# Norm steps, key parts, latent copies and the last two latent heads of a streaming encoder step, rearranged

## The chip, the cores and the metric

The kernel runs on one core of one Trainium2 chip. The metric is the device time of one execution in microseconds (us). The core has a matmul engine (TensorE, PE in the profile; PEld are its weight loads, which overlap the matmuls), three engines for elementwise work (VectorE: DVE, ScalarE: ACT, GpSimd: POOL), and SyncE (SP), whose queue issues most DMA transfers. Each engine takes its own instructions in order and waits on semaphores for the others.

## The reference

One layer of an encoder is applied to two streams: a prompt of 16 meta tokens and 512 rows, and a sample of 64 new rows with 128 cached rows behind it. Width 2048, float32. The core of it:

```python
h = rmsnorm(x, norm_attn_g)
qd, kd, vd, qm, ckv, krope = project(h)           # one matrix w_in; norms and rope on the latent parts
# 8 differential heads, two softmaxes each
p = softmax(qd0 . kd0 + bias) - lam * softmax(qd1 . kd1 + bias)
o_d = rmsnorm(p @ vd, diff_subln_g) * (1 - lam_init)
# 8 latent heads: keys and values expanded from ckv
km, vm = expand_latent(ckv)
o_m = softmax((qn . km + qr . krope) * scale) @ vm
x = x + concat(o_d, o_m) @ w_out
h = rmsnorm(x, norm_ffn_g)
x = x + (silu(h @ gate) * (h @ up)) @ down
y = rmsnorm(x, final_norm_g)                      # also returned: new keys, values, latents, roped keys
```

Keys are visible by chunks of 64 rows.

## The kernel before

Rows are kept as columns: an operand tile is 128 features by up to 592 tokens (64 sample rows, 512 prompt rows, 16 meta rows). For float32 accuracy every operand is split into a high part (ScalarE copies it to a rounded type, lines 156 and 160) and a low part (VectorE subtracts, lines 153 and 161); a product is three matmuls, high-high, high-low and low-high (`mm3`, line 183). Weights arrive by DMA in a tile `wr`, and are split into `wh` and `wl`.

The work has these stages.

- Start (lines 361 to 518): the input is loaded, turned by TensorE in 16 blocks (`transpose_x`), split, and multiplied with the first head's query and key weights block by block (`project_both`). Loads are issued by SyncE in the order of lines 407 to 413. In blocks 11 and 12 two products for the bias table ride along (`bias_part`), in block 15 a transpose of the gains (`gains_part`); VectorE copies both out of the spare half of the block's PSUM tile. After block 13 the row factors of the first norm are worked out on VectorE and ScalarE (`rc`, lines 502 to 506); `row_factors` then spreads them with ten small matmuls (`prb`) and a VectorE copy (`rb`). It stands behind block 14. After block 15 comes the value projection of head 0 (`psv`).
- Eight differential heads (lines 537 to 771): for each head three projections of 16 blocks (96 matmuls each). Between their blocks runs the attention of the head before. `new_keys` evacuates the key projection and stacks high and low halves (`stack_keys`, two parts for each of two ranges); `keys` and `natural` turn keys for the output. `diff_attend` makes scores into two banks ("sp"), which VectorE reduces (line 626) and ScalarE exponentiates (line 630), then calls `probabilities_times_values`, then squares the output, sums it by TensorE (`pq`), applies a reciprocal root (`rsqrt`, lines 165 to 169) and the gain (line 669).
- Latents (lines 773 to 893): norm and rope of the latent rows; five times three transposes `pn` go through the single bank "tp", are copied by VectorE (`nn`, line 882) and stored.
- Latent heads and first half of the mixing (lines 918 to 1110): eight heads (`latent_attend`), each with scores and then `probabilities_times_values` through the banks "tp" (one) and "po" (one). A head's values wait for the whole chain of the head before (`att2[h - 1]`, line 1081). `mix_out` multiplies the differential outputs with the first half of `w_out`; it has the last rank, and so fills what the heads leave.
- Second half of the mixing (lines 1250 to 1301): latent outputs are read back (`m`, three buffers with tag "x"), split to `mh` and `ml`, and multiplied (line 187); the first gate weights `raw0` are loaded.
- The feed-forward layer (from line 1303): gate, up and down products in a Winograd form, then the last norm.

TensorE's order up to line 1115 is planned when the program is built: `Streams` runs generators against a planned clock `now`, which only TensorE's instructions advance. A generator yields a planned time to wait, a list of others to wait for, or takes a PSUM bank (`take`) that another gave back with a delay (`give`). Of those ready, the one with the lowest rank goes on. TensorE's instructions are pinned in that order by `keep_in_program_order` (an instruction is issued after all that was traced before it on its engine; it need not wait for them to finish). The other engines' instructions, and the DMA issues, are ordered by a scheduler at build time, by its own estimate of when each is ready.

## Time and profile before

| | us |
|---|---|
| median of 3 runs | 2391.92 (2391.61 to 2392.06) |
| profiled execution | 2392.82 |
| its span, first to last instruction | 2390.9 |
| mean granted TensorE clock | 0.995 |

Windows of the profile are in us from the span's start. Roughly, the start takes 0 to 55, the differential heads 55 to 480, the latents to 530, the latent heads to 771, the second half of the mixing to 875, and the feed-forward layer the rest.

A row of the timeline has the start, the duration, engine, line, operation, the tiles written and read, their shapes, the count of instructions merged in it, and in brackets how long the engine had been idle and which instruction released it. A row of the windows has the stretch, its length, and for each engine its busy time and its number of instructions, then the granted TensorE clock (1.00 is full), the DMA share and GB/s. A row of the waits has who waited for whom, the total, the number and the longest. Matmuls are pipelined, so the durations of neighbours overlap.

### The profile page before, as it was taken

To read this page: it belongs to the slowest core of one execution; us is meant where nothing else is said; L and a number is where in the kernel's file an instruction comes from. 1 tells how busy PE (TensorE), PEld (TensorE's weight loads), DVE (VectorE), ACT (ScalarE), POOL (GpSimd) and SP (SyncE) were. 2 spreads that over 40 slices of the span, in tenths; PEclk is the share of its full clock that TensorE was granted. 3 is DMA by queue.
4 is the path that set the end of the run, shared out by engine and by line. 5 is a ranking of instruction groups with operands and counts; after the bars stand their busy time and mean duration, and the time that the engine had idled before them with its cause. 6 is when DMAs were issued, how large, how long until landed. Compare 5 with 4: busy or idle time off the path is not lost. (4 is left out here: it accounts for less than half of the span.)

```text
span 2390.9 us, 43556 instructions
## 1 busy us (share of the span) xinstructions
PE 2341.0 (98%) x17318; PEld 2304.9 (96%) x17318; DVE 1883.8 (79%) x2742; ACT 1128.1 (47%) x2000; POOL 738.6 (31%) x457
## 2 busy tenths in 40 slices
PE   8999999999998999999999999999999999999998
PEld 7999999989998999999999999999999999999997
DVE  6566777676674789888888888888888788899884
ACT  6454555344454554444444444444444333333435
POOL 1000000130000455555555554554554222222220
PEclk9999999999999999999999999999999999999999
DMA  9432333263323643444345345445445984654522
GB/s 277 110 92 83 93 98 94 66 177 104 113 86 124 185 146 119 141 156 160 126 156 165 128 149 166 132 145 166 139 139 185 321 284 152 231 172 151 189 89 97
DMA packets 361513, 353.09 MB, mean 148 GB/s; under 512 B 23719, under 2 KB 318414, under 8 KB 361310
## 3 DMA queue, kind: packets, MB, share of 16 engines
q1 hardware_dynamic: 359038, 345.78, 45.8%
q0 software_dynamic: 992, 3.48, 0.5%
q8 instruction: 136, 2.23, 0.4%
q10 hardware_dynamic: 1280, 1.06, 0.2%
q14 instruction: 67, 0.55, 0.1%
HBM read 268.82 MB, written 82.34 MB: 147 GB/s over the span
## 5 line engine op out<-in xcount | busy, mean ns | idle before, releaser
L1240 PE MATMUL m<-b,wh 128*128 128x288 f32 x7280 | 1061.9, 294 | 7.0 <-ACT wh L156 3.7
L1240 PEld LDWEIGHTS m<-b,wh 128*128 128x128 f32 x7280 | 995.5, 188 | 10.2 <-ACT wh L156 6.8
L1244 PE MATMUL m<-b,wl 128*128 128x288 f32 x3640 | 583.0, 296 | 3.7 <-DVE wl L153 2.7
L153 DVE TENSOR_TENSOR wl<-raw,wh 128x1024 fp32r<-128x1024 f32 (+2 forms) x347 | 511.1, 1474 | 39.4 <-ACT wh L156 37.3
L1244 PEld LDWEIGHTS m<-b,wl 128*128 128x128 f32 x3640 | 514.4, 188 | 9.2 <-DVE wl L153 8.2
L156 ACT ACTIVATE wh<-raw 128x1024 fp32r<-128x1024 f32 (+2 forms) x347 | 313.5, 904 | 364.5 <-PE m L1240 318.7
L1226 POOL TENSOR_TENSOR ws<-raw 128x512 f32<-128x512 f32 (+2 forms) x124 | 226.9, 1830 | 614.9 <-DVE wl L153 367.5
L156 ACT ACTIVATE wh<-ws 128x512 fp32r<-128x512 f32 (+2 forms) x248 | 196.6, 793 | 286.0 <-PE m L1240 120.0
L153 DVE TENSOR_TENSOR wl<-ws,wh 128x512 fp32r<-128x512 f32 (+2 forms) x248 | 249.9, 1008 | 8.1 <-PE m L1244 4.4
L108 PE MATMUL ps<-xh,wh 128*128 128x296 f32 (+1 forms) x992 | 223.9, 307 | 2.2 <-DVE ls L635 1.2
L108 PE MATMUL ps<-xl,wh 128*128 128x296 f32 (+1 forms) x992 | 216.4, 300 | 0.2
L108 PE MATMUL ps<-xh,wl 128*128 128x296 f32 (+1 forms) x960 | 208.3, 298 | 0.5 <-DVE wl L153 0.5
L1390 DVE TENSOR_TENSOR c<-c,s 128x288 fp32r<-128x288 f32 x172 | 171.2, 995 | 0.0
L108 PEld LDWEIGHTS ps<-xh,wh 128*128 128x128 f32 x992 | 161.1, 191 | 5.7 <-ACT wh L156 2.6
L1498 DVE TENSOR_TENSOR y<-y,m 128x288 f32<-128x288 f32 x280 | 125.8, 450 | 49.8 <-PE m L1244 49.7
L108 PEld LDWEIGHTS ps<-xl,wh 128*128 128x128 f32 x992 | 161.7, 190 | 1.1 <-DVE xl L161 1.0
L108 PEld LDWEIGHTS ps<-xh,wl 128*128 128x128 f32 x960 | 156.4, 190 | 0.7 <-DVE wl L153 0.7
L1226 POOL TENSOR_TENSOR raw<-raw 128x1024 f32<-128x1024 f32 (+1 forms) x46 | 141.8, 3084 | 3.5
L153 DVE TENSOR_TENSOR wl<-wr,wh 128x1024 fp32r<-128x1024 f32 (+1 forms) x109 | 115.7, 1061 | 33.1 <-ACT wh L156 30.4
L156 ACT ACTIVATE wh<-wr 128x1024 fp32r<-128x1024 f32 (+1 forms) x111 | 101.8, 917 | 75.7 <-PE ps L108 55.8
L1336 DVE TENSOR_TENSOR c<-c,m 128x288 f32<-128x288 f32 x171 | 73.2, 448 | 79.3 <-PE m L1244 40.6
L1409 POOL TENSOR_TENSOR c<-c,rb 128x576 f32<-128x576 f32 x44 | 74.8, 1699 | 138.0 <-ACT c L1408 138.0
(363 smaller groups left out, 3022.0 us busy)
## 6 DMA issues: line engine op xcount, KB each, us to landing
raw<-in_ffn_w_gate SPq DMA_DIRECT2D x44, 1024.0 KB, 6.1
raw<-in_ffn_w_up SPq DMA_DIRECT2D x44, 1024.0 KB, 7.7
b<-opspill SPq DMA_DIRECT2D x147, 288.0 KB, 6.1
raw<-in_ffn_w_down SPq DMA_DIRECT2D x32, 1024.0 KB, 5.4
wr<-in_w_in SPq DMA_DIRECT2D x57, 512.0 KB, 4.0
opspill<-s SPq DMA_DIRECT2D x43, 576.0 KB, 3.1
opspill<-c SPq DMA_DIRECT2D x43, 576.0 KB, 6.8
raw<-in_ffn_w_down SPq DMA_DIRECT2D x8, 1280.0 KB, 6.2
```

What stands on the lines that cost most here:

```text
L108: self.tc.keep_in_program_order(self.pe.matmul(out, lhsT, rhs, start=start, stop=stop))
L153: V.tensor_tensor(lo, src, f32(hi), op=ALU.subtract)
L156: S.activation(hi, src, AF.Copy)
L1226: (G if p in (5, 7) else V).tensor_tensor(x, y, z, op=ALU.add if p == 5 else ALU.subtract)
L1240: PE.matmul(banks[p], wh[:, k, :], x, start=first and new and k == 0 and x is hi, stop=False, skip_group_check=not new)
L1244: PE.matmul(banks[p], wl[:, k, :], hi, start=False, stop=last and k == n - 1, skip_group_check=not new)
L1336: V.tensor_tensor(c, c, banks[p], op=ALU.add)
L1390: V.tensor_tensor(src[:, k].bitcast(F32R), src[:, k], f32(hi[:, k]), op=ALU.subtract))
L1409: G.tensor_tensor(g[:, f, :], g[:, f, :], rb2, op=ALU.mult)
L1498: V.tensor_tensor(c, c, banks[p], op=ALU.add)
```

## The change

- The second weight group is loaded ahead of the last 1024 columns of the own rows, the one-hot table and the bias. `row_factors` goes behind block 15. The copies of bias and gains go behind the block's split and copy.
- In heads 0 to 6 the three VectorE steps of the output norm and the gain are each issued 2.0 of planned time apart, and pinned behind what was traced on VectorE before (`rsqrt_apart`, `behind`). The parts of `stack_keys` move from `new_keys` into `keys`, 1.0 apart, their subtractions pinned likewise. The bank of `natural`'s first transposes is given back after 2.9 in place of 1.9.
- The copy `nn` is made by ScalarE.
- The weights of the first mixing block are asked for at block 11 of the last projection (`late`).
- The last latent head waits for the head before the one before it, and goes beside head 6: it uses the banks "sp" and "ps" in place of "tp" and "po", the freed query tiles `cqh` and `cql` for its buffers, a `pm` of its own (cleared by GpSimd), and steps 2.0 of planned time apart.
- In the second half of the mixing four of the eight input tiles use the four buffers "xg"; the load of `raw0` is pinned behind what SyncE was given before.

The diff, cut to its core:

```diff
+    def behind(ins):
+        return tc.keep_in_program_order(ins)
+
+    def rsqrt_apart(r, v, pace):
+        S.activation(r, v, AF.Ln)
+        S.activation(r, r, AF.Exp, scale=-0.5)
+        yield pace
+        behind(V.tensor_tensor(v, v, r, op=ALU.mult))
+        yield pace
+        behind(V.scalar_tensor_tensor(v, v, -0.5, r, op0=ALU.mult, op1=ALU.mult))
+        yield pace
+        behind(V.scalar_tensor_tensor(r, v, 1.5, r, op0=ALU.add, op1=ALU.mult))
+        yield pace
...
-    def project(ps, wsrc, xs, ready=None, n=TH):
+    def project(ps, wsrc, xs, ready=None, n=TH, late=None):
...
+                if late and kc == 11:
+                    late()
                 yield 0
...
+    def rotating(pool):
+        def made(name, cols):
+            if name == "p5x":
+                return pool.tile([P, cols], F32R, name=name)
+            return [pool.tile([P, cols], F32R, name=name + s, tag="pk" + s, bufs=2) for s in "hl"]
+        return made
...
                 if cg == 1:
+                    load_own(slice(512, 1024), load)
+                load_both(4 * cg, 4, (load, load))
+                if cg == 1:
+                    load_own(slice(1024, D), load)
                     load(oh, c_onehot)
                     load(rbt, rel_bias)
-                    load_own(slice(512, D), load)
-                load_both(4 * cg, 4, (load, load))
...
-                if kc in (11, 12):
-                    bias_part(kc - 11, spare)
-                elif kc == KC - 1:
-                    gains_part(spare)
+                rider = {11: bias_part, 12: bias_part, KC - 1: gains_part}.get(kc)
+                if rider:
+                    rider(kc - 11, spare)
                 xt = xn.tile([P, T], F32, name="xt", tag=f"xt{kc % 12}")
                 split_scaled(xh[kc], xl[kc], sp, gA[:, kc:kc + 1])
                 V.tensor_copy(xt, sp)
                 store(xspill[kc], xt[:, 0:TQ])
+                if rider:
+                    {bias_part: bias_row, gains_part: gains_out}[rider](kc - 11, spare)
...
-                if kc == KC - 2:
-                    row_factors()
+            row_factors()
...
-            st.give("tp", 1.9)
+            st.give("tp", 2.9)
...
-            yield 2.0
+            for new, old in NEW:
+                for part in stack_keys(kk, new, z[:, old]):
+                    yield 1.0
+            yield 1.0
...
-                V.tensor_tensor(kk[c][half[1 - c], cols], src[half[c]], f32(kk[c][half[c], cols]), op=ALU.subtract)
+                behind(V.tensor_tensor(kk[c][half[1 - c], cols], src[half[c]], f32(kk[c][half[c], cols]),
+                                       op=ALU.subtract))
+                yield
...
-            rsqrt(r, sq)
-            V.scalar_tensor_tensor(o32, o32, g08, r, op0=ALU.mult, op1=ALU.mult)
             if h < H - 1:
+                yield from rsqrt_apart(r, sq, 2.0)
+                behind(V.scalar_tensor_tensor(o32, o32, g08, r, op0=ALU.mult, op1=ALU.mult))
                 store(mspill[h], o32)
+            else:
+                rsqrt(r, sq)
+                V.scalar_tensor_tensor(o32, o32, g08, r, op0=ALU.mult, op1=ALU.mult)
...
-                for new, old in NEW:
-                    stack_keys(kk[h % 2], new, z[:, old])
...
-                    yield from project(ps, w_in[:, off:off + P], xs1, n=QH if i < 4 else TH)
+                    yield from project(ps, w_in[:, off:off + P], xs1, n=QH if i < 4 else TH,
+                                       late=(lambda: mixed.append(mix_weights(0))) if i == 3 else None)
...
-                V.tensor_copy(nn[0:n], pn[0:n, 0:320])
+                S.activation(nn[0:n], pn[0:n, 0:320], AF.Copy)
...
-                wh, wl = weights(w_out[0:1024, i * P:(i + 1) * P].rearrange("(k p) c -> p k c", p=P), 8, P)
+                wh, wl = mixed.pop() if mixed else mix_weights(i)
...
-            yield [valued[h // 2]] + ([att2[h - 1]] if h else [])
+            beside = h == H - 1
+            yield [valued[h // 2]] + ([att2[h - 1 - beside]] if h else [])
...
+            if beside:
+                home = lambda tag, dtype: aq[0].tile([P, TQ], dtype, name="pv" + tag, tag=tag)
+
+                def made(name, cols):
+                    if name == "p5x":
+                        return aq[0].tile([P, cols], F32R, name=name, tag="e", bufs=2)
+                    return [home(f"cq{s}{name[2]}", F32R)[:, 0:cols] for s in "hl"]
+
+                o32, pm = home("cql3", F32), home("cqh3", F32R)[0:80, 0:512]
+                banks = ("sp", sbank), ("ps", lambda: pjt()[:, 0])
+                G.memset(f32(pm), 0.0)
+            else:
+                o32, pm = zx.tile([P, TQ], F32, name="o32", tag="o32"), shared["pm"]
+                made, banks = rotating(aq[0]), (("tp", tbank), ("po", obank))
             yield from probabilities_times_values(
...
-                o32, 2, {})
+                pb, p5, pm, shared["vm"][:, c], [(vh[:, 1 + t, c], vl[:, 1 + t, c]) for t in range(4)],
+                vh[:, 0, c], (vh[:, 5, c], vl[:, 5, c]), made, *banks, 2.0 if beside else 0.0,
+                o32, {})
...
-        m = ma.tile([P, TQ], F32, name="x", tag="x", bufs=3)
+        m = ma.tile([P, TQ], F32, name="x", **(dict(tag="xg", bufs=4) if 3 <= h < 7 else dict(tag="x", bufs=3)))
...
-            raw0 = load_raw(rw, w_gate, 0, 8, 0, 1, "ws")
+            raw0 = load_raw(rw, w_gate, 0, 8, 0, 1, "ws",
+                            lambda dst, part: tc.keep_in_program_order(nc.sync.dma_start(dst, part)))
```

In `probabilities_times_values` the pool and bank arguments become `made` (which hands out the split tiles) and two pairs of a bank's name and its maker; its steps are the same.

More of the change, by code (lines that the diff above doesn't have):

```diff
@@ L227, in stack_own, with probabilities_times_values @@
         V.tensor_tensor(v[NS:P], src, f32(v[0:NS]), op=ALU.subtract)
-    def probabilities_times_values(pt_b, p5, pm, vm, vkeys, vown, vpast, pool, tbank, pso, pace, o32, bufs, transposed):
+    def probabilities_times_values(pt_b, p5, pm, vm, vkeys, vown, vpast, made, tbank, pbank, pace, o32, transposed):
         def evac(name, src, rows, cols):
-            hi = pool.tile([P, cols], F32R, name=name + "h", tag="pkh", bufs=bufs)
-            lo = pool.tile([P, cols], F32R, name=name + "l", tag="pkl", bufs=bufs)
+            hi, lo = made(name, cols)
             split(hi[0:rows], lo[0:rows], src[0:rows, 0:cols])
@@ L239, in times_values @@
                 PE.matmul(po[:, c0:512], a, b, start=False, stop=(n == 3 and m == 2))
-        yield from st.take("po")
-        po = pso.tile([P, 512], F32, name="po", tag="po")
-        yield from st.take("tp")
-        tp = tbank()
+        yield from st.take(pbank[0])
+        po = pbank[1]()
+        yield from st.take(tbank[0])
+        tp = tbank[1]()
         for b in range(4):
@@ L250, in probabilities_times_values @@
         last = []
-        st.give("tp", 2.2)
+        st.give(tbank[0], 2.2)
         for t in range(2):
             yield pace
-            yield from st.take("tp")
+            yield from st.take(tbank[0])
             w = 512 - P * t
-            tp = tbank()
+            tp = tbank[1]()
             for b in range(t, 4):
@@ L264, in probabilities_times_values @@
             last = [(t, (hi, lo), t * P)]
-            st.give("tp", 2.2)
+            st.give(tbank[0], 2.2)
         yield pace
-        yield from st.take("tp")
-        tp = tbank()
+        yield from st.take(tbank[0])
+        tp = tbank[1]()
         for n, (t, b) in enumerate(((2, 2), (2, 3), (3, 3))):
@@ L274, in probabilities_times_values @@
         last = [(2, (hi[:, 0:256], lo[:, 0:256]), 256), (3, (hi[:, 256:384], lo[:, 256:384]), 384)]
-        st.give("tp", 1.7)
+        st.give(tbank[0], 1.7)
         yield pace
-        yield from st.take("tp")
-        tp = tbank()
+        yield from st.take(tbank[0])
+        tp = tbank[1]()
         for n in range(2):
             PE.transpose(tp[:, n * P:(n + 1) * P], p5[:, n * P:(n + 1) * P], ident)
-        p5x = pool.tile([P, 2, 2, NS], F32R, name="p5x")
+        p5x = made("p5x", 4 * NS).rearrange("p (a b c) -> p a b c", a=2, b=2)
         split(p5x[:, 0], p5x[:, 1], tp[:, 0:2 * P].rearrange("p (a b) -> p a b", a=2)[:, :, 0:NS])
@@ L286, in probabilities_times_values @@
         S.activation(o32[:, NS:TQ], po, AF.Copy)
-        st.give("tp", 1.7)
-        st.give("po", 1.2)
+        st.give(tbank[0], 1.7)
+        st.give(pbank[0], 1.2)
         yield pace
-        yield from st.take("po")
-        po5 = pso.tile([P, 512], F32, name="po", tag="po")
+        yield from st.take(pbank[0])
+        po5 = pbank[1]()
         vh, vl = vpast
@@ L298, in probabilities_times_values @@
         V.tensor_tensor(o32[:, 0:NS], o32[:, 0:NS], po5[:, NS:2 * NS], op=ALU.add)
-        st.give("po", 1.0)
+        st.give(pbank[0], 1.0)
+    def rotating(pool):
[4 more added lines that the diff above has]
+        return made
     def ev(ps, n=TH):
@@ L340, in tbank, with obank @@
             return pst.tile([P, 512], F32, name=name, tag="tp")
+        def obank(name="po"):
+            return pso.tile([P, 512], F32, name=name, tag="po")
         def ztile(name="z"):
@@ L427, in bias_part, with bias_row @@
                 PE.matmul(bank[0:H], rbt, oh[:, cols[i]], start=True, stop=True)
+            def bias_row(i, bank):
                 trs = ztile("trs")[0:H, 0:NREL // 2]
@@ L433, in bias_part, with gains_part, gains_out @@
                         G.dma_start(tsk[h], trow[h:h + 1, :].to_broadcast([P, NREL]))
-            def gains_part(bank):
+            def gains_part(i, bank):
                 PE.transpose(bank[:, 0:P], gains, ident)
+            def gains_out(i, bank):
                 V.tensor_copy(gT, bank[:, 0:rows])
@@ L567, in keys @@
             PE.transpose(pk[:, 0:P], ck, ident)
-            stack_keys(kk, slice(T, TP), pk[:, 0:P])
+            for part in stack_keys(kk, slice(T, TP), pk[:, 0:P]):
+                pass
             st.give("tp", 1.5)
@@ L1084, in latent_attend @@
             c = slice(i * P, (i + 1) * P)
-            o32 = zx.tile([P, TQ], F32, name="o32", tag="o32")
+            if beside:
[10 more added lines that the diff above has]
+                made, banks = rotating(aq[0]), (("tp", tbank), ("po", obank))
             yield from probabilities_times_values(
-                pb, p5, shared["pm"], shared["vm"][:, c], [(vh[:, 1 + t, c], vl[:, 1 + t, c]) for t in range(4)],
-                vh[:, 0, c], (vh[:, 5, c], vl[:, 5, c]), aq[0], tbank, pso, 0.0,
-                o32, 2, {})
+                pb, p5, pm, shared["vm"][:, c], [(vh[:, 1 + t, c], vl[:, 1 + t, c]) for t in range(4)],
+                vh[:, 0, c], (vh[:, 5, c], vl[:, 5, c]), made, *banks, 2.0 if beside else 0.0,
+                o32, {})
             store(mspill[8 + h], o32)
```

7 lines of the change are left out of this document (5 added, 2 removed).

## The prediction

> **What bounds the kernel now.** I read the page's first part, then the table of stages, then TensorE's waits, then the short stretches around them.
>
> ```profile
> span 2390.9 us, 43556 instructions
> ...
> PE 2341.0 (98%) x17318; PEld 2304.9 (96%) x17318; DVE 1883.8 (79%) x2742; ACT 1128.1 (47%) x2000; POOL 738.6 (31%) x457
> ```
>
> TensorE is the bound: 49.9 us of 2390.9 are left without a matmul, and the change removes no matmul. It can only win back idle time, and time in which matmuls ran slowly. The table of stages says where these are (columns: stretch, length, then busy time and instructions of PE, PEld, DVE, ACT, POOL, then granted clock, DMA share, GB/s).
>
> ```profile
> 0.00:60.00 60.00, 49.44 (x326) 45.74 (x327) 39.83 (x65) 36.41 (x75) 8.80 (x22) 0.97 0.92 277
> ...
> 190.00:205.00 15.00, 11.61 (x74) 11.31 (x74) 11.68 (x30) 7.22 (x17) 0.00 (x0) 0.89 0.25 75
> 205.00:505.00 300.00, 298.56 (x2218) 294.30 (x2218) 210.35 (x467) 150.40 (x313) 25.88 (x22) 1.00 0.36 100
> 505.00:530.00 25.00, 19.93 (x125) 17.65 (x125) 17.81 (x26) 9.15 (x15) 6.50 (x7) 0.93 0.53 141
> ...
> 744.00:782.00 38.00, 31.74 (x194) 27.84 (x193) 15.20 (x25) 14.50 (x27) 0.00 (x0) 0.87 0.51 161
> ...
> 930.00:2391.00 1461.00, 1445.13 (x10773) 1430.55 (x10771) 1244.92 (x1454) 665.82 (x1035) 613.12 (x333) 1.00 0.50 163
> ```
>
> Four short stretches (start, 190 to 205, 505 to 530, 744 to 782) hold 25.3 us of the idle time and all of the lowered clock. The feed-forward part from 930 on idles 15.9 us, and the change does not touch it. TensorE's waits name the causes (who waits for whom: us, times, longest).
>
> ```profile
> PE pn L112 <- DVE nn L882: 3.6, 3, 1.9
> PE sp L108 <- DVE nm L626: 3.4, 1, 3.4
> ...
> PE prb L108 <- DVE rc L169: 2.5, 1, 2.5
> ...
> PE ps L108 <- DVE wl L153: 1.9, 2, 1.5
> ...
> PE ps L108 <- DVE ls L635: 1.2, 1, 1.2
> ...
> PE pnb L112 <- ACT na L564: 0.5, 1, 0.5
> ```
>
> **The clock doubles some of these waits.** The half-clock stretches lie on one grid of 3.41 us; so I asked for the stretches of that grid.
>
> ```profile
> 47.81:51.23 3.42, 0.95 (x9) 0.80 (x8) 1.88 (x7) 1.33 (x6) 1.14 (x5) 1.00 0.93 334
> 51.23:54.64 3.41, 3.41 (x17) 3.41 (x16) 1.53 (x2) 0.00 (x0) 0.00 (x0) 0.50 1.00 363
> 194.59:198.00 3.41, 1.91 (x15) 1.67 (x13) 3.29 (x5) 1.44 (x4) 0.00 (x0) 1.00 0.56 154
> 198.00:201.41 3.41, 1.52 (x10) 1.52 (x11) 2.91 (x12) 1.35 (x5) 0.00 (x0) 1.00 0.53 168
> 201.41:204.83 3.42, 3.42 (x16) 3.36 (x15) 1.76 (x7) 1.38 (x5) 0.00 (x0) 0.50 0.00 0
> ...
> 447.17:450.58 3.41, 3.41 (x27) 3.41 (x26) 3.16 (x9) 0.73 (x2) 0.00 (x0) 1.00 0.62 161
> ...
> 522.27:525.68 3.41, 1.66 (x9) 0.93 (x9) 3.38 (x7) 1.45 (x3) 0.00 (x0) 1.00 0.68 197
> 525.68:529.09 3.41, 3.41 (x16) 3.41 (x16) 2.42 (x4) 0.00 (x0) 0.00 (x0) 0.50 0.67 193
> ...
> 768.03:771.44 3.41, 1.84 (x13) 1.38 (x11) 1.03 (x3) 2.22 (x6) 0.00 (x0) 1.00 0.03 9
> 771.44:774.85 3.41, 3.15 (x14) 3.11 (x14) 1.58 (x3) 0.96 (x3) 0.00 (x0) 0.50 0.84 273
> ```
>
> Idle for 2.47, 1.89, 1.75 or 1.57 us of 3.41 (length less PE busy), and the next stretch runs at 0.50. Idle for 1.50 (194.59 to 198.00), and the next is at 1.00. A half-clock stretch gets through 16 matmuls where a full one gets through 27, so it costs 11/27 of 3.41, about 1.4 us. A wait of some 1.6 us in one stretch thus costs 1.6 plus 1.4.
>
> [...]
>
> **The change part by part.**
>
> *Order of the first loads (lines 407 to 413).*
>
> ```profile
> 20.16 1.04 ACT L156 ACTIVATE wh<-wr 128x1024 fp32r<-128x1024 f32 x1
> ...
> 21.25 0.54 PE L108 MATMUL ps<-xh,wh 128*128 128x288 f32 x2 [1.00 <-ACT wh L156]
> ```
>
> The two transfers of the second weight group move ahead of two thirds of the own rows, the one-hot table and the bias on SyncE's queue: four issues (oh, rbt, two of xo) go behind two of wr, some 0.4 MB, which at the 277 GB/s of the first stage is 1.5 us. The split at 20.16 stands behind ScalarE's squares, without an idle mark before it, so its place in the queue decides and not the data alone. TensorE lost 1.00 us there and 0.46 for the other half (the 1.9 of the waits less its longest). Between 0 and 1.5; I take **1.0**, as an earlier transfer lets the scheduler put the split earlier. What goes later is read from the eighth block on, over 8 us on.
>
> *Row factors one block later (lines 507 to 508), bias and gain copies behind the splits.*
>
> ```profile
> 47.56 0.43 PE L108 MATMUL ps<-xh,wl 128*128 128x296 f32 x2
> 50.46 1.69 PE L108 MATMUL prb<-ident,rc 128*128 128x128 f32 x10 [2.47 <-DVE rc L169]
> 52.19 0.78 DVE L445 COPY rb<-prb 128x592 f32<-128x592 f32 x1 [1.87 <-PE prb L108]
> ...
> 54.82 0.44 PE L108 MATMUL ps<-xh,wh 128*128 128x296 f32 x2
> ```
>
> Block 14 ended at 47.99. Block 15's twelve products, 1.5 us by the 27 in 3.41 and some 0.3 until the last is out, fill most of the wait to 50.46; the factors then start near 50.4. Their ten matmuls took 1.69 partly at half clock; I take 1.2. New: the value projection comes right behind, and its bank is probably the one that the factors leave, so it waits for the 0.78 us copy, 0.9 with its start. It starts at 52.5 in place of 54.82: **2.3**, with the clock in it (3.2 if the bank is another; 1.5 if the chain is late by 0.8). The copies moved (0.5 us each on VectorE) are the same work later, behind a split that TensorE needs first.
>
> *Norm steps and key parts at a distance (lines 167 to 169, 577, 668 to 669, 700 to 701).*
>
> ```profile
> 194.32 0.75 DVE L167 TENSOR_TENSOR sq<-sq,r 128x576 f32<-128x576 f32 x1
> ...
> 199.40 0.43 DVE L626 CUSTOM_DVE_ANT_0 e<-sp,bias 128x272 f32<-128x272 f32 x1
> ```
>
> Between these, VectorE ran four norm steps and four key subtractions in a row, and the score reduction, whose matmuls were done by then, stood behind them. Both score banks were full, and TensorE waited 3.40. With steps 2.0 and key parts 1.0 of planned time apart, each kept behind what was traced before it, the reduction goes ahead of them: 3.40 and one half-clock stretch, at most 4.8; I take **4.6**. The added planned time (some 8 us for a norm, 3 for keys) ends in nothing urgent: the norm's result is only stored, for the mixing stage, and keys are wanted when the value projection's 96 matmuls are done, some 12 us by the 27 in 3.41 above. The 1.2 us of ps on ls (an evacuation behind norm steps) may go or stay: **0.6**. The longer lease of the transpose bank (2.9 for 1.9) takes away most of the 0.5 before pnb: **0.4**.
>
> *Turned latents copied by ScalarE (line 882), first mixing weights asked for at block 11 (line 921).*
>
> ```profile
> 509.57 0.76 DVE L761 TENSOR_TENSOR zl<-ps,rb 128x576 f32<-128x576 f32 x1 [0.83 <-PE ps L108]
> ...
> 511.38 5.06 DVE L161 SCALAR_TENSOR_TENSOR cql<-zl,gT,cqh 128x576 fp32r<-128x576 f32 x4
> 516.36 0.47 DVE L882 COPY nn<-pn 80x320 f32<-80x320 f32 x1
> ...
> 521.29 1.06 ACT L156 ACTIVATE wh<-wr 128x1024 fp32r<-128x1024 f32 x1 [8.86 <-PE ps L108]
> ...
> L564 ACT ACTIVATE na<-pna x8: 572/580/601, 62.8 to 395.0; 128x512 f32<-128x512 f32 x8
> ```
>
> The copy stands behind 5.06 us of VectorE work while ScalarE idles for 8.86 us. On ScalarE it costs about the same (the last row, from the view of line 564: eight copies of 128x512, 572 to 601 ns) and starts when its transposes are done. All 3.6 us of waits on nn go, and the stretch at 525.68. What is late next: VectorE's four splits now end near 516, and the query products that read them come near 520. The first mixing weights' low half, traced a third of a projection earlier, can be made in VectorE's 0.8 us hole before 509.57: 1.3 of 1.45. Together 1.3 + 3.6 + 1.4 = 6.3; I take **6.0**.
>
> *Last two latent heads side by side (line 1081 on).* The same window view, of the mixing products' tile alone and then of everything:
>
> ```profile
> 744.28:758.90 14.62, 9.46 (x68) 8.98 (x66) 1.51 (x2) 0.00 (x0) 1.00 0.71 225
> ...
> 744.28:758.90 14.62, 13.19 (x99) 12.53 (x97) 5.49 (x9) 4.71 (x9) 0.00 (x0) 1.00 0.71 225
> 758.99:770.94 11.95, 7.70 (x34) 5.42 (x33) 3.24 (x8) 4.74 (x11) 0.00 (x0) 0.71 0.07 26
> ```
>
> Head 6's chain (six steps of transposes, split, products) runs among the mixing products: 13.19 - 9.46 = 3.7 us of matmuls are its own. Head 7's chain, the same work, then runs alone for 11.95 us, with a wait at each step and two of its three and a half stretches at half clock. Side by side: 9.46 + 2 x 3.7 = 16.9 from 744.28, so 761.2 in place of 770.94, and 771.44 to 774.85 at full clock: at most 9.7 + 1.4. Against it: head 7's output takes one of the two "ps" banks, so the last mixing block must wait for its predecessor's evacuation (0.75 us and its waits); and when mixing runs out, the last steps are bare again, for 2 to 3 us. I take **8.5**. Mixed-in cost: one clearing of 80 rows on GpSimd, idle there; head 7's tiles use freed query tiles. The further input buffers and the gate load moved past the second stage's first blocks on SyncE's queue: nothing; that load is read only after the second stage's sixteen blocks.
>
> Sum: 1.0 + 2.3 + 4.6 + 0.6 + 0.4 + 6.0 + 8.5 = 23.4. The planner's whole order behind each edit shifts, and new meetings of the 1.2 us kind are as likely as old ones; I charge two, 2.4. Net **21**. The profiled execution took 2392.82 us (span 2390.9 and 1.9 around it), 0.9 over the median 2391.92; from the median, **2371**.
>
> **Rivals.**
>
> 1. *The chains meet instead of overlapping*: ps banks and ScalarE's order string them out, and half of the gain is left, 4.5 for 8.5: 2375. For it: each step of the bare chain took about 2 us for 0.6 of matmuls. Against: 9.46 us of filler.
>
> 2. *The waits move.* Keys and norm steps spread into the next score blocks; seven heads pay about 1.5 us each, 10 us: 2381. Against: VectorE is busy 210 of 300 us from 205 to 505 (the table of stages), so there are holes.
>
> 3. *The clock is not the gaps' doing.* If a lowered clock needs a longer idle, the six half-clock stretches stay, 6 x 1.4 = 8.4 off: 2379. [...]
>
> 4. *Slower: the kept order blocks VectorE.* Ten or so instructions of each head are now pinned behind all traced before; one that waits for ScalarE holds score reductions and weight splits behind it, and TensorE waits. At 2.9 us a head over eight heads the gain is gone; at 4 it is 32 - 21: 2403. For it: each key subtraction reads what ScalarE has just written (line 576). Against: later instructions may still be scheduled ahead of a pinned one.
>
> **How the numbers follow.** Forecast 0.57 (own range 2365 to 2376), rival 1 0.17, rival 2 0.10, rival 3 0.04, nearly all given back 0.06, rival 4 0.06. Ends: all upper values (1.5, 3.2, 4.8, 1.2, 0.5, 6.3, 11.1: 28.6) give 2363; rivals 1 and 2 together some 2384. Range 2362 to 2384. A difference under 0.2% (4.8 us) can't be told from none: faster 0.88, same 0.06, slower 0.06.
>
> **What would show it.** Right: no wait of pn on nn, none over 1 us of sp on nm in the heads, factors without a 2.5 us wait but a wait of about 0.9 behind them, no 0.50 clock between 60 and 800, the second part's first product (line 187) some 8 us less after the last scores than now. Wrong: new waits of TensorE on VectorE between 60 and 450, or the last chain still alone for over 6 us.

## The result and the profile after

The changed kernel took 2376.26 us (median of 6 runs, 2373.45 to 2378.03) against 2391.77 before (2390.82 to 2392.28): ratio 0.9935, 95% interval 0.9922 to 0.9947. That is 15.5 us less; the forecast was 21 less. Run five times more, it gave 2375.54; over all eleven runs the median is **2375.7**, and the experiments are set against that. The profiled execution, 2373.45, is the fastest of the eleven, so its trace shows a little more gain than the kernel usually has.

The first part of its page:

```profile
span 2371.7 us, 43559 instructions
...
PE 2333.7 (98%) x17318; PEld 2300.8 (97%) x17318; DVE 1877.4 (79%) x2737; ACT 1130.8 (48%) x2005; POOL 735.1 (31%) x458
```

The same 17318 matmuls; 38.0 us without one (span less PE) where there were 49.9. PE is also busy 7.3 us less, mostly slow matmuls that became full-speed ones: up to its last matmul the kernel before has six stretches of 3.41 us at clock 0.50, the changed one two, 13.7 us fewer. To see where, I cut both spans at the same events: first value product, first mixing product, first query product of the latent heads, first product of the mixing's second half, first product of the feed-forward layer. Kernel before, table of stages (columns as before: stretch, length, busy time of each engine, clock, DMA):

```profile
0.00:54.82 54.82, 44.26 (x289) 40.56 (x289) 34.88 (x58) 31.37 (x67) 8.80 (x22) 0.97 0.92 276
54.82:509.37 454.55, 449.03 (x3329) 443.38 (x3328) 311.15 (x692) 230.68 (x481) 29.49 (x30) 1.00 0.36 100
509.37:525.43 16.06, 10.99 (x70) 8.71 (x68) 12.18 (x15) 5.49 (x8) 3.96 (x3) 1.00 0.58 148
525.43:770.94 245.51, 237.09 (x1745) 230.99 (x1744) 152.79 (x354) 109.12 (x255) 8.23 (x12) 0.98 0.36 108
770.94:877.67 106.73, 105.44 (x768) 103.51 (x769) 83.17 (x120) 60.23 (x119) 51.58 (x46) 0.98 0.59 178
877.67:2390.89 1513.22, 1494.18 (x11126) 1477.73 (x11124) 1289.61 (x1506) 691.18 (x1074) 636.58 (x344) 1.00 0.49 162
```

Changed kernel, the same cuts:

```profile
0.00:51.06 51.06, 42.14 (x288) 39.18 (x289) 34.73 (x59) 32.21 (x67) 8.77 (x22) 0.99 0.93 283
51.06:502.02 450.96, 449.18 (x3328) 443.55 (x3329) 309.19 (x689) 229.80 (x476) 25.05 (x31) 1.00 0.37 102
502.02:512.92 10.90, 10.32 (x69) 8.78 (x68) 10.48 (x14) 7.52 (x14) 3.01 (x2) 1.00 0.52 133
512.92:750.24 237.32, 232.11 (x1746) 228.00 (x1745) 152.79 (x354) 110.53 (x258) 8.80 (x13) 1.00 0.38 114
750.24:858.09 107.85, 104.75 (x768) 102.12 (x769) 81.00 (x120) 59.86 (x119) 50.88 (x46) 1.00 0.60 180
858.09:2371.68 1513.59, 1495.17 (x11126) 1479.18 (x11124) 1289.20 (x1507) 690.83 (x1074) 638.60 (x344) 1.00 0.49 162
```

Length against length: start 3.8 us less, differential heads 3.6, latents 5.2, latent heads 8.2; the mixing's second half 1.1 more, the feed-forward layer 0.4 more. In each of the first four stages PE's idle time (length less busy) fell: 10.6 to 8.9, 5.5 to 1.8, 5.1 to 0.6, 8.4 to 5.2.

TensorE's waits in the changed kernel, the rows that answer to the forecast:

```profile
PE m L201 <- ACT mh L156: 2.0, 3, 0.9
...
PE ps L108 <- DVE xo L976: 1.2, 1, 1.2
...
PE pna L112 <- DVE kk L612: 1.0, 1, 1.0
...
PE pn L112 <- ACT nn L921: 0.6, 1, 0.6
...
PE sp L108 <- DVE nm L663: 0.4, 1, 0.4
```

Of 3.6 us of pn on nn 0.6 is left, of 3.4 us of sp on nm 0.4. The second row is new, and the third was 0.2 before. Of the first, one wait of 0.9 stood before too; the others, 0.62 and 0.52, are new: the second half of the mixing now comes at the latent heads' last outputs sooner than these are read back (ScalarE waited 2.62 and 1.43 us for the transfers of `x`). But the wait for the row factors did not go. The timeline of the start:

```profile
45.69 0.21 ACT L165 ACTIVATE rc<-ss 128x5 f32<-128x5 f32 x1 [0.68 <-DVE ss L537]
...
45.94 1.06 ACT L156 ACTIVATE wh<-wr 128x1024 fp32r<-128x1024 f32 x1
46.91 0.19 ACT L166 ACTIVATE rc<-rc 128x5 f32<-128x5 f32 x1
47.03 1.23 DVE L153 TENSOR_TENSOR wl<-wr,wh 128x1024 fp32r<-128x1024 f32 x1 [1.38 <-ACT wh L156]
...
48.57 0.17 DVE L169 SCALAR_TENSOR_TENSOR rc<-ss,rc 128x5 f32<-128x5 f32 x1
...
48.88 1.31 PE L108 MATMUL prb<-ident,rc 128*128 128x128 f32 x10 [2.70 <-DVE rc L169]
...
50.23 0.77 DVE L476 COPY rb<-prb 128x592 f32<-128x592 f32 x1 [1.50 <-PE prb L108]
...
51.06 0.62 PE L108 MATMUL ps<-xh,wh 128*128 128x296 f32 x1 [0.87 <-DVE rb L476]
```

Between the two ScalarE steps of the root (0.2 us each) now stands a weight split of 1.06, and before VectorE's three steps its other half, 1.23. It is the last group of the value weights. The factors wait 2.70, although block 15 has already run; and behind them the value projection waits 0.87 for the bank.

### The profile page after: what moved, and what is told of

It is laid out like the page before. It is cut to its first block, busy times and chain, and to the rows that moved or that the text cites. A ratio compares the mean times of both kernels' runs of the same rounds, so it can differ in the third digit from the quotient of the medians.

```text
span 2371.7 us, 43559 instructions
## 1 busy us (share of the span) xinstructions
PE 2333.7 (98%) x17318; PEld 2300.8 (97%) x17318; DVE 1877.4 (79%) x2737; ACT 1130.8 (48%) x2005; POOL 735.1 (31%) x458
## 3 DMA queue, kind: packets, MB, share of 16 engines
q10 hardware_dynamic: 1280, 1.06, 0.2%
```

## The experiments

Each is the changed kernel with one edit, timed beside the kernel before, whose medians in the four sittings were 2390.97, 2391.66, 2391.49 and 2392.71. Each has five runs, "keys at once only" four. Only in the third sitting (the unedited kernel and the repeats of the first two edits) does the changed kernel itself stand beside them; the others are set against its 2375.7 across sittings. One edited kernel's runs in one sitting spread over 1.4 to 5.6 us, and the nine of the kernel before over 3.4 to 7.5, so a difference below some 2 us between two kernels settles nothing by itself; then the trace has to say it.

| edit | median us | ratio to before, 95% | against 2375.7 |
|---|---|---|---|
| none, again | 2375.54 | 0.9932 (0.9920 to 0.9945) | |
| split kept behind the root | 2372.59 and 2373.03 | 0.9922 (0.9910 to 0.9935), 0.9923 (0.9911 to 0.9935) | -3.1 (ten runs: 2372.6) |
| row factors ahead of block 15 | 2373.10 and 2371.18 | 0.9921 (0.9909 to 0.9934), 0.9918 (0.9904 to 0.9931) | -3.5 (ten runs: 2372.2) |
| old order of loads | 2378.17 | 0.9944 (0.9931 to 0.9956) | +2.5 |
| norm in a row, keys at once | 2382.18 | 0.9963 (0.9950 to 0.9977) | +6.5 |
| keys at once only | 2377.39 | 0.9941 (0.9928 to 0.9955) | +1.7 |
| nn on VectorE | 2382.03 | 0.9962 (0.9950 to 0.9975) | +6.3 |
| mixing weights as before | 2373.17 | 0.9924 (0.9911 to 0.9938) | -2.5 |
| last two heads one after the other | 2381.63 | 0.9966 (0.9953 to 0.9978) | +5.9 |
| split behind the root, cached keys not pinned | 2373.15 | 0.9922 (0.9908 to 0.9935) | -2.5 |

**The split in the root's steps.** The root is written out, and the last split may be issued only after its last ScalarE and VectorE steps:

```diff
-                    rsqrt(rc, ss)
+                    S.activation(rc, ss, AF.Ln)
+                    rooted = S.activation(rc, rc, AF.Exp, scale=-0.5)
+                    V.tensor_tensor(ss, ss, rc, op=ALU.mult)
+                    V.scalar_tensor_tensor(ss, ss, -0.5, rc, op0=ALU.mult, op1=ALU.mult)
+                    refined = V.scalar_tensor_tensor(rc, ss, 1.5, rc, op0=ALU.add, op1=ALU.mult)
...
-            split_both(5)
+            with tc.issue_after(rooted.ins), tc.issue_after(refined.ins):
+                split_both(5)
```

> The changed kernel, with the split of the last value weights kept behind the row factors' chain on ScalarE and VectorE (nothing left out). Theory: in the changed kernel this split stands between the chain's steps (1.06 us on ScalarE, 1.23 on VectorE), so TensorE waits 2.70 us for the factors and 0.87 for the copy, and a half-clock stretch follows. Then the wait for the factors falls to 0.5 to 1.0 us, the half-clock stretch near 50 goes, and the time falls by 2.0 + 1.4 = 3.4 us, to about 2373. The run to run spread of the changed kernel (2373.5 to 2378.0) should shrink as well if it comes from how many half-clock stretches these two waits set off. Rival: the chain is late for another reason (the sums of squares come late); then the wait stays above 2 us and the time within 1 us of 2376.

> The last value weights' split kept behind the root's steps, again. Theory: the wait before prb falls from 2.7 to near 0.6 and the half-clock stretch behind it goes, 2.5 to 4 below the unedited run of this call. Rival, that the spread made the difference: within 1 of it.

It measured 2372.59, and 2373.03 the second time. The start in the second run's trace:

```profile
48.22 1.31 PE L108 MATMUL prb<-ident,rc 128*128 128x128 f32 x10 [0.79 <-DVE rc L542]
...
50.42 0.54 PE L108 MATMUL ps<-xh,wh 128*128 128x296 f32 x2 [0.88 <-DVE rb L476]
```

0.79 in place of 2.70, and the 0.88 behind it, as my forecast had them. The two together, 1.67, lie partly in one stretch of the grid (46.75 to 50.16, idle for 1.41), and no half-clock stretch follows: the next, from 50.16 on, is at 1.00. (The first run's trace has 0.62 and 0.89.) In this sitting the gain beside the unedited run was 2.5, the low end of what was expected. So the wait is the split's doing. One expectation failed: the spread of the runs did not shrink, 4.2 and 4.6 us here against 4.6 in the first six runs of the changed kernel.

**The row factors ahead of block 15.** Was the move worth its 2.3 us, and only hidden by the split?

```diff
                 project_both(kc)
...
-            row_factors()
+                if kc == KC - 2:
+                    row_factors()
```

> The row factors stand ahead of block 15 again, everything else as changed. My theory: what I forecast of this step (2.3 us) did not come, because the split of the last value weights now falls between the steps of the root (1.06 us of ScalarE and 1.23 us of VectorE), and that is due to the order in which the scheduler sees the work, not to block 15. If so, undoing the move costs little or nothing: 2375 to 2377 (between -1 and +1). Rival: the move itself is worth its 2.3 us and only the split hides it; then the wait before prb grows by block 15's 1.5 us and a second half-clock stretch comes: 2378 to 2379.

> The row factors ahead of block 15, again. The first time it measured 2373.1, 3.2 less than the changed kernel, though its profile shows the value projection starting near 53 in place of 51.06. If the move behind block 15 costs by itself (my forecast was a gain of 2.3), this stays 2 to 4 below the unedited run of this call. If the difference was the spread of the runs, it lies within 1 of it.

Neither of the first two theories expected what came: 2373.10, which is 2.6 below the eleven runs' median, then 2371.18, 4.4 below the unedited run beside it. By whole runs, undoing the move saves some 3.5 us. The second sitting's trace:

```profile
46.62 2.27 PE L108 MATMUL prb<-ident,rc 128*128 128x128 f32 x10 [2.33 <-DVE rc L169]
...
48.62 0.83 PE L108 MATMUL ps<-xh,wh 128*128 128x288 f32 x2
```

With the factors traced ahead of block 15, ScalarE and VectorE do the root's steps first, and the split only at 50.95 and 52.04. The wait is 2.33, less than the 2.70 it has with block 15 in front. And the second row has no bracket: block 15 follows at once, in a bank of its own, and it covers the copy of `rb`, for which the value projection waited 0.87 us in the changed kernel. In the first sitting's trace the wait is 2.75.

Is it the move that costs, then, or the split that came with it? The traces tell, counted from the end of block 14 (us, two traces each but for the kernel before); the 61st value product stands behind every half-clock stretch of the start.

| kernel | to the factors | to the value projection | to its 61st product |
|---|---|---|---|
| before | 2.47 | 6.82 | 15.45 |
| changed | 4.42, 4.42 | 6.60, 7.64 | 16.17, 17.57 |
| factors ahead of block 15 | 2.75, 2.33 | 7.95, 6.73 | 16.49, 14.93 |
| split held behind the root | 2.34, 2.51 | 4.54, 4.70 | 12.84, 13.01 |

**In the start the move gains, and the split turns it into a loss.** With the split held, the value projection comes 2.3 and 2.1 us sooner after block 14 than before the change, and its 61st product 2.6 and 2.4 sooner: the forecast's 2.3. Against the factors ahead of block 15, where the split also comes behind the root, the 61st product is 2.8 sooner by the means. With the split free, the 61st product is 0.7 and 2.1 us later than before the change, and from 1.1 to 2.6 in the five edited kernels below that leave loads and start alone. By the means, undoing the move saves 1.2 of its 3.5 here. Up to the feed-forward layer nothing is left of that: it begins at 860.73 and 856.59 with the factors ahead of block 15, at 858.09 and 858.66 in the changed kernel. The rest stands in the feed-forward layer, which the edit doesn't touch: 1511.77 and 1512.69 us against 1513.59 and 1515.20. About 1.4 of that (an estimate: such a stretch of 3.41 us holds 16 matmuls for the 27 of a full one) is a half-clock stretch near 1856, which the changed kernel's two traces have and these two don't; why the layer is shorter by more over whole runs stays open.

**The loads of the start.** The old order of lines 407 to 413.

```diff
                 if cg == 1:
-                    load_own(slice(512, 1024), load)
-                load_both(4 * cg, 4, (load, load))
-                if cg == 1:
-                    load_own(slice(1024, D), load)
                     load(oh, c_onehot)
                     load(rbt, rel_bias)
+                    load_own(slice(512, D), load)
+                load_both(4 * cg, 4, (load, load))
```

> The start loads in their old order (own rows, one-hot table and bias ahead of the second weight group), everything else as changed. My theory: the two waits of block 1 on its weights (1.0 and 0.5 us) return, and what follows in the start is later by as much: 2377.3 to 2378 (1.0 to 1.5 more than the changed kernel's 2376.3). Rival: the wait for the first rows, which also was shorter in the changed kernel's profile, is what set the start, and the order of the later loads only shifts where TensorE idles: 2376 to 2376.6.

It measured 2378.17, 2.5 more. The two waits are back to the hundredth:

```profile
20.50 0.54 PE L108 MATMUL ps<-xh,wh 128*128 128x288 f32 x2 [1.00 <-ACT wh L156]
...
21.76 0.54 PE L108 MATMUL ps<-xh,wl 128*128 128x288 f32 x2 [0.46 <-DVE wl L153]
```

1.46 of the 2.5 stands there; the rest, within the spread, may be the wait for the factors, 3.4 in this trace, with three half-clock stretches in a row behind it (50.77 to 61.02) where the changed kernel's traces have one and two.

**Norm steps and key parts.** First both undone, then the key parts alone.

```diff
-                yield from rsqrt_apart(r, sq, 2.0)
-                behind(V.scalar_tensor_tensor(o32, o32, g08, r, op0=ALU.mult, op1=ALU.mult))
+                rsqrt(r, sq)
+                V.scalar_tensor_tensor(o32, o32, g08, r, op0=ALU.mult, op1=ALU.mult)
...
-            for new, old in NEW:
-                for part in stack_keys(kk, new, z[:, old]):
-                    yield 1.0
-            yield 1.0
+            yield 2.0
...
+                for new, old in NEW:
+                    stack_keys(kk[h % 2], new, z[:, old])
...
-            st.give("tp", 2.9)
+            st.give("tp", 1.9)
```

(`stack_keys` then yields nothing and pins nothing. The second kernel has all but the first four lines.)

> The changed kernel, with the norm steps in a row, the key parts at once and unpinned, and the transpose bank given back after 1.9 again. Theory: the 3.4 us wait of scores on the score reduction near 200 comes back with its half-clock stretch, and the 1.2 us near 446; the new 0.98 us wait near 75 goes: the time rises by 4 to 5 us, to 2380 to 2381. Rival: the wait near 200 was a meeting that an earlier start moves anyway; then it does not come back, and the time stays within 1.5 us of 2376 or falls.

> Only the key parts as before (all four in new_keys, not pinned, the bank's lease 1.9); the norm steps stay 2.0 apart and pinned. Undoing both cost 5.9 us, with the 3.4 us wait of sp on nm near 200 back. Theory: the norm's steps in a row are what held the score reduction, since they take 0.75 us each and a subtraction 0.4 us; then this alone costs 1 to 2 (the wait at 446 and the bank's), no wait over 1.5 us near 200: 2377 to 2378.5. Rival: it is the four subtractions in a row, or both together, and the wait near 200 returns with its half-clock stretch: 2380 to 2382.

Both undone cost 6.5; TensorE's waits there:

```profile
PE sp L108 <- DVE nm L657: 3.4, 1, 3.4
...
PE ps L108 <- DVE zn L986: 2.3, 1, 2.3
...
PE ps L108 <- DVE ls L666: 1.2, 1, 1.2
```

The first and the last are the waits of the kernel before, returned as they were; a half-clock stretch follows the first, at 200.10, and one the second, at 527.78. With the keys alone undone, 1.7 more, and:

```profile
PE ps L108 <- DVE zn L986: 3.0, 1, 3.0
...
PE sp L108 <- DVE nm L657: 2.1, 5, 1.1
```

The waits of `sp` on `nm` are five over all the heads, none over 1.1, and no half-clock stretch stands near 200. So it is the norm's row that did the damage, as the first theory said; by the difference the spaced norm is worth 4.8 and the spaced keys 1.7. Spacing the keys also spares the latents: 3.0 and 2.3 stand here at the place where the changed kernel waits 1.2 (`ps` on `xo`). How the one brings the other I did not follow.

**The turned latents on VectorE again.**

```diff
-                S.activation(nn[0:n], pn[0:n, 0:320], AF.Copy)
+                V.tensor_copy(nn[0:n], pn[0:n, 0:320])
```

> The changed kernel, with the five turned latent tiles copied by VectorE again. Theory: the waits of the latent transposes come back behind VectorE's four query splits (3.6 us before the change) with one half-clock stretch, less the 1.2 us that the changed kernel waits there now for an evacuation: the time rises by 3 to 5 us, to 2379 to 2381. Rival: the asked-for-sooner mixing weights alone took away most of it, VectorE being earlier by a microsecond: the time rises by less than 1.5 us.

It measured 2382.03, 6.3 more, a little past the range. Its timeline:

```profile
507.86 4.16 DVE L161 SCALAR_TENSOR_TENSOR cql<-zl,gT,cqh 128x576 fp32r<-128x576 f32 x4
...
511.95 0.47 DVE L921 COPY nn<-pn 80x320 f32<-80x320 f32 x1
...
512.48 0.44 PE L112 MATMUL pn<-ident,zl 128*128 128x128 f32 x2 [3.75 <-DVE nn L921]
```

The copy stands behind four VectorE splits and TensorE waits 3.75 for it in one piece, more than the 1.9 at most in the kernel before; that the mixing products now come earlier, with less left to fill in front of it, is the likely reason, not a shown one.

**The first mixing weights asked for as before.** The `late` argument is left out, so the first mixing block asks for its weights itself.

```diff
-                                       late=(lambda: mixed.append(mix_weights(0))) if i == 3 else None)
+                                       late=None)
```

> The first mixing weights asked for where they were before, with the first mixing block itself, everything else as changed. Theory (forecast's step, 1.3 of the 6.0 for this stage): the first mixing products wait 1.3 to 1.5 us for the low half of their weights again, and since about 1.5 of a 3.41 us stretch is the edge at which the next stretch runs at half clock, at most 1.4 more: 2377 to 2378.5 beside 2375.7, the median of the eleven runs of the changed kernel so far. Rival: with ScalarE making the turned latents, VectorE is free at that place and the weights are there in time anyway: 2375 to 2376.3.

It measured 2373.17: no loss, and the rival was right that the weights are there anyway.

```profile
500.25 1.21 DVE L153 TENSOR_TENSOR wl<-wr,wh 128x1024 fp32r<-128x1024 f32 x1
...
503.90 0.43 PE L108 MATMUL ps<-mxh,wh 128*128 128x288 f32 x2
```

The low half is ready near 501.5, the first mixing product starts at 503.90 and waits for nothing. The 2.5 us below the changed kernel do not stand in the stages that the edit could change: the waits there are the same (0.58 and 1.22), and the feed-forward layer begins at 858.96, later than in the changed kernel's two traces (858.09 and 858.66). They stand in that layer, 1512.46 us against 1513.59 and 1515.20. Its longest wait, 2.1 us in both kernels, falls into one stretch of the clock's grid in the changed kernel (first row) and over two in this one (second row):

```profile
1852.77:1856.18 3.41, 1.30 (x11) 1.10 (x10) 3.41 (x8) 0.63 (x1) 1.67 (x2) 1.00 1.06 395
...
1851.60:1855.01 3.41, 2.03 (x14) 1.62 (x12) 3.41 (x6) 0.95 (x2) 2.68 (x2) 1.00 1.04 387
```

The stretch after the first is at 0.50, the one after the second at 1.00. So the edit itself shows neither loss nor gain.

**The last two heads one after the other.**

```diff
-            beside = h == H - 1
+            beside = False
```

> The changed kernel, with the last latent head behind head 6 again, on the banks tp and po. Theory: the side by side chains are the largest term, 8.5 us and one to three half-clock stretches; the time rises by 8.5 to 11 us, to 2385 to 2387, and the last chain shows alone for about 12 us again. Rival (chains only string out): the time rises by 4.5 us or less, to 2381 or below.

It measured 2381.63, 5.9 more, between the two expectations. Head 7's chain alone, from the last mixing product to the first product of the second half:

```profile
742.87:760.60 17.73, 11.58 (x53) 8.54 (x51) 5.46 (x13) 6.10 (x14) 0.00 (x0) 0.64 0.24 79
```

17.73 us for 53 matmuls, at a mean clock of 0.64. In the trace its part from the first query product to the feed-forward layer is 9.2 longer than the changed kernel's, but its run only 6.9; 2.7 came back in the feed-forward layer, of which a half-clock stretch near 1856, present in the one and absent in the other, is 1.4.

**The cached keys not pinned.** The new wait of `pna` on `kk` looked like rival 4: a pinned subtraction behind a weight split. With the split behind the root as above, and (`stack_keys` takes its way of pinning as an argument, left at `behind` elsewhere)

```diff
-            for part in stack_keys(kk, slice(T, TP), pk[:, 0:P]):
+            for part in stack_keys(kk, slice(T, TP), pk[:, 0:P], lambda ins: ins):
```

> As changed, with the last split kept behind the root's steps (that alone measured 2372.6), and the subtraction of the cached keys no longer pinned behind what was traced before it on VectorE. Theory: the wait of pna on kk at 75.30 (0.98 us) comes from the pin, one instruction that had to stay behind a weight split; without it the wait goes, and 1.0 to 2.5 is saved besides, where a lowered clock hung on it: 2370 to 2371.6. Rival: the scheduler, left free, puts the subtraction where it holds something else, as it did in the kernel before, and the gain is nil or lost: 2372.5 to 2374.

It measured 2373.15, no better than the split alone. The wait stands where it was:

```profile
74.29 1.23 DVE L153 TENSOR_TENSOR wl<-wr,wh 128x1024 fp32r<-128x1024 f32 x1 [1.03 <-ACT wh L156]
...
75.55 0.29 DVE L617 TENSOR_TENSOR kk<-pck,kk 64x128 fp32r<-64x128 f32 x1
...
75.99 0.63 PE L112 MATMUL pna<-ident,z 128*128 128x128 f32 x4 [1.00 <-DVE kk L617]
```

The scheduler puts the split first even when nothing makes it. My reading of that row as the pin's doing was wrong.

**The changed kernel again**, for its spread:

> The changed kernel once more, nothing edited, so that its own spread is known beside the next two. My theory: its times depend on how many half-clock stretches a run meets (a wait of 1.5 to 3 us falls inside one stretch of the grid or over two, and each half-clock stretch is 1.4 us) and on when the first weights land; the median is 2375 to 2377 as before, over a spread of 4 us or more, and a profile that is not the fastest run shows at least one half-clock stretch more than the first profile's two inside the span. Rival: the first six times were high by chance and the kernel's median is 2373 to 2374; then neither of the next two is faster than it.

2375.54, over 2374.13 to 2376.26: narrower than expected (2.1 us for 4 or more), at the expected place. Its profile has two half-clock stretches at the start where the first profile has one, as expected.

## Why the prediction was right, and where not

The direction and the bound were right: TensorE's idle time in four short stretches, with the six stretches at clock 0.50 that lie in them. Of the forecast 21 us 15.5 came: inside the range 2362 to 2384, at the upper end of the forecast's own 2365 to 2376. The number alone would fit rival 1 (2375) better than the forecast; the traces show that its mechanism did not occur. One reading was too wide: not all of the lowered clock lay in the four stretches, as the kernel before also was at half clock from 2385.94 to its end, 4.9 us without a matmul, which the change doesn't touch. By steps, what undoing each one cost by whole runs:

| step | forecast | by undoing |
|---|---|---|
| order of the first loads | 1.0 | 2.5 |
| row factors one block later | 2.3 | -3.5 (1.2 of it in the start) |
| norm and keys apart, with the bank's lease | 5.6 | 6.5 |
| nn on ScalarE | 4.7 | 6.3 |
| first mixing weights sooner | 1.3 | none seen (-2.5 by times, in the feed-forward layer) |
| last two heads side by side | 8.5 | 5.9 |
| new meetings | -2.4 | in the rows above |
| sum | 21.0 | 17.7, without the fifth row |

The sum of the parts, 17.7 (or 15.2 with the fifth row's times), stands by the 16.1 of the whole (2391.8 less 2375.7) within the spread. That does not show the parts to be independent: each row is uncertain by some 2 us, and each holds a share of the feed-forward layer, which took between 1510.85 and 1515.20 us in the fourteen traces though no edit touches it.

- **The step that failed** is "Row factors one block later". I wrote that block 15 would "fill most of the wait", with the root's steps going on beside it as before. I named the bank that the value projection would wait for, and it did, 0.87 for my 0.9. What I left out is that the root's small steps have their place in ScalarE's and VectorE's queues only by the scheduler's choice. Moved behind block 15, they met a weight split of 1.06 and 1.23 us. It took back what block 15 hid. With the split held back the wait is 0.79 and 0.62, and the value projection comes 2.3 and 2.1 us sooner after block 14 than before the change, as forecast; with the split free its 61st product comes 0.7 and 2.1 later. So the sum of the step was right, and the order of the other engines, which it took for given, was not. The 3.5 by whole runs overstates the loss: in the traces 1.2 stands in the start, and 2.2 in the feed-forward layer, which the step doesn't touch.
- **Rival 3** (the clock is not the gaps' doing) falls. Before, five half-clock stretches stood between 190 and 775; the changed kernel's two traces have none between 60 and 800, and they came back with their waits: near 200 with the norms in a row, near 513 with nn on VectorE, from 748 on with the heads apart. (Four of the edited kernels have one near 757, behind the new waits on `mh`; with the split held back it begins at 756.72.)
- **Last two heads**: the price of the stage was right. From 744.28 to 770.94 before, 26.66 us; the same work took 18.15 (732.09 to 750.24 in the changed kernel), 8.5 less. But the stage behind it then paid 1.1 more, and over whole runs 5.9 is seen, with a feed-forward layer 2.7 shorter in the undone kernel's trace.
- **nn on ScalarE** was under-sized by 1.6, **the first mixing weights** over-sized by 1.3: with VectorE rid of work the split found its hole without help.
- **New meetings**: two were charged at 1.2 each. Two came, 0.98 (`pna` on `kk`) and 1.22 (`ps` on `xo`), and two smaller ones on `mh`, 0.62 and 0.52.
- **Rivals 1, 2 and 4**: the chains did overlap; norm and key steps in the heads brought back one wait of 1.0, not one a head; and no pinned instruction was found to block VectorE.
- **The signs**: of those for right, no long wait of `sp` on `nm`, no half clock between 60 and 800, the 0.87 behind the factors and the 8.5 us at the second part came; a wait of `pn` on `nn` stayed (0.6, now on ScalarE), and the wait for the factors did not go (2.70). Of those for wrong, one came: the new wait of TensorE on VectorE at 75, 0.98 us, which the pin did not cause.

A version faster than both: the changed kernel with the row factors ahead of block 15, 2372.2 over ten runs, or with the split held behind the root, 2372.6. Up to the feed-forward layer the second is the sooner (it begins at 857.01 and 856.73, against 860.73 and 856.59); by their times they are equal. The two edits were not run together.

## What to carry to other kernels

Before work is put in front of a wait to fill it, look at what else the scheduler may then put into the chain that is waited for: small steps on two engines can be lost between splits of a us each (here steps of some 0.2, and splits of 1.06 and 1.23), unless their order is pinned. Long rows of elementwise steps that nothing waits for are worth spacing out when something short that TensorE waits for shares their engine (here 4.8 us for the norm's). And a wait is to be priced by the stretch that it falls in: here the same wait of 2.1 us was followed by a half-clock stretch, by estimate 1.4 us more, in some traces and not in others. Where an edit is worth a few us of two thousand, look also at the stages that it does not touch before its time is put down to it.

## What the runs showed of the hardware

**The grid lies differently from run to run.** The start of the repeat of the changed kernel, on its own grid (columns as above; the clock is the third number from the end):

```profile
44.80:48.21 3.41, 0.71 (x6) 0.49 (x5) 1.68 (x5) 1.36 (x3) 2.40 (x7) 1.00 0.57 182
48.21:51.62 3.41, 2.54 (x11) 2.33 (x12) 1.04 (x2) 0.00 (x0) 0.00 (x0) 0.50 1.02 397
51.62:55.04 3.42, 3.42 (x15) 3.42 (x16) 3.34 (x5) 2.82 (x5) 0.00 (x0) 0.50 1.00 307
```

And the same place in the first profile of the same kernel:

```profile
47.12:50.53 3.41, 1.31 (x10) 1.19 (x10) 1.84 (x5) 0.00 (x0) 1.16 (x5) 1.00 0.87 306
50.53:53.95 3.42, 2.89 (x12) 2.89 (x13) 3.30 (x5) 2.05 (x3) 0.00 (x0) 0.50 1.03 356
53.95:57.36 3.41, 3.41 (x27) 3.41 (x27) 3.31 (x7) 2.37 (x5) 0.00 (x0) 1.00 0.91 268
```

The same two waits, 2.70 and 0.87, fall into other stretches: two at half clock in the one, one in the other. Counted from the end of block 14, the 61st value product comes 1.4 us later in the one than in the other (17.57 and 16.17). The wait in the feed-forward layer shown above is a second such place: a half-clock stretch follows it, between 1855 and 1866, in seven of the fourteen traces. They are part of the spread and not all of it: with the two waits of the start shortened and no half clock there, the runs still spread over 4.2 and 4.6 us. The longest single gap in these rows is 2.70 us.

**Idle time is not the whole of it.** I had read the edge as some 1.5 us of idle, from the kernel before (1.50 idle, and the next stretch at 1.00; 1.57, and the next at 0.50). Two edited kernels speak against that as a rule. The split held back, second sitting:

```profile
753.31:756.72 3.41, 2.09 (x10) 1.36 (x10) 1.78 (x3) 1.48 (x3) 0.00 (x0) 1.00 0.67 247
756.72:760.14 3.42, 3.42 (x16) 3.42 (x16) 2.23 (x5) 1.85 (x3) 1.75 (x2) 0.50 0.78 238
```

The cached keys not pinned:

```profile
48.07:51.49 3.42, 1.85 (x15) 1.64 (x14) 2.46 (x9) 1.36 (x3) 1.34 (x5) 1.00 0.72 264
51.49:54.90 3.41, 2.53 (x20) 2.38 (x19) 3.31 (x5) 1.24 (x2) 0.00 (x0) 1.00 1.04 404
```

Idle for 1.32 with 10 matmuls, and the next stretch is at 0.50; idle for 1.57 with 15, and it stays at 1.00. I then counted the matmuls begun in each full-clock stretch that idled over 1.15 us, in fourteen traces (both kernels and all edits), from 9 to 2300 us: with 10 or fewer, 28 of 29 were followed by half clock; with 11, 2 of 3; with 12 or more, 1 of 44. In the kernel before and the first profile of the changed kernel alone it is 7 of 7 with 10 or fewer and none of 10 with 12 or more; there idle time parts them too (1.57 and over, 1.50 and under). (By that count, of those begun, the two stretches shown have 9 and 13.) So in these traces the count of matmuls begun parts the cases better than idle time does. It was found afterwards in traces made for other questions, and no run was made to test it.

**When the weights land also differs from run to run.** In the same trace of the cached keys' kernel, early in the start:

```profile
17.46 1.06 ACT L156 ACTIVATE wh<-wr 128x1024 fp32r<-128x1024 f32 x1 [2.75 <-DMA wr<-in_w_in]
```

ScalarE stood 2.75 us for a weight transfer with the next block's split queued behind it, TensorE lost 1.61 at 19.82 and met a half-clock stretch (its pairs of products of 296 columns start 0.49 and 0.50 us apart from 21.76 on, and 0.28 and 0.27 apart from 16.72 on), and the value projection began at 52.86. With the split held back alone, the same instructions in the start, it began at 48.58 and 50.42. How much of the spread this makes, no run shows.
